# Reordering the end of the first layer norm: which plain tile comes first, which engine makes the low parts, and one square's scratch

## The chip, the cores and the metric

The kernel runs on one core of a Trainium2 chip. The metric is the device time of one execution in microseconds (us). The time before is 1299.06 us, the median of three runs.

## The reference, cut to what matters

One encoder layer over 1056 rows (1024 of a prompt, 32 of a running stream) of width 1024: a combined projection, a gated convolution beside a sparse attention, an output projection, a layer norm, an MLP with squared ReLU and a second layer norm.

```python
mix = jnp.concatenate([conv_out, attn], axis=-1) @ w_o
x = _layernorm(ALPHA * x + mix, ln1_g, ln1_b)
hid = jax.nn.relu(x @ w_ff1)
ff = (hid * hid) @ w_ff2
x = _layernorm(ALPHA * x + ff, ln2_g, ln2_b)
```

`_layernorm` subtracts the mean over the 1024 features, divides by the root of the variance plus 1e-5, and applies a gain and an offset. This case is about the first layer norm (whose result the kernel calls x1) and the start of `x @ w_ff1`.

## The kernel before

**Layout.** Features lie on partitions, rows of x on the free axis, so x is eight tiles of 128 features by 1056 columns; four buffers `z[0]` to `z[3]` hold two of them each. Columns are handled in three chunks (`CHUNKS`: 0 to 384, 384 to 768, 768 to 1056) for the output projection and the norm, and in halves of 528 and quarters of 264 for the MLP. A float32 product is made of three reduced-precision ones: every operand is split into a high part (a copy on ScalarE, `split` at L108 or its like) and a low part (raw minus high, a subtraction on VectorE or GpSimd, L111 or its like), and TensorE adds high by high, high by low and low by high (`dense` at L131 to L133, `three` at L875 to L877).

**The stretch of the change.** After the attention, the jobs in `MID` run: `w0d` the output projection of chunk 0 for the feature tile d, `lcd` the parts of the norm of chunk c, `xc` writes chunk c of x1 (`x1_out`), `tt` calls `combine_x1`, and `fce` makes the product of the plain tile e with the quarter c of x1 (`ff1`). There are four plain tiles (hidden features 14, 30, 15, 31 in groups of 128) and four quarters, so 16 products, each 24 matmuls of 264 columns over 8 feature tiles. Quarters 0 and 1 are columns 528 to 1056, quarters 2 and 3 columns 0 to 528. Quarters 2 and 3 take columns of chunk 0, which is normalised last, so ten of the products stand behind `x00` and `tt` in `MID`: four of the first two tiles (f20 f30 f21 f31), and six of the third and the fourth.

**The norm of chunk 0.** `ln_var_pe` centres each `z[i]` on VectorE (L658), squares it on ScalarE into a scratch (L660), and TensorE adds the squares over the features with a matrix of ones (`total`, L674). The scratches are named `junka`, `tie`, `rank`, `tie`, so the fourth square takes the second's place. Then come the root (L686), the reciprocal (L687), the scaling of the four buffers (L690), and `x1_out`: high parts on ScalarE (L797), gain and offset (L801), low parts on GpSimd for even tiles and VectorE for odd ones (L804), and a store of the four buffers (L806).

**The sums of x1.** The MLP's other hidden features go through a scheme of seven products instead of eight, which needs four sums of x1's blocks: t1 to t4. `combine_x1` makes them in place on VectorE (L839, L840, L841, L848; eight instructions over 128 x 1056), and `split_sum` splits each into a high part on ScalarE (L833) and a low part (L834): eight instructions of each, of which VectorE has four low parts (both of t2, the second of t3 and of t4) and GpSimd four (both of t1, the first of t3 and of t4).

**Buffers.** A product of `ff1` takes one of six PSUM buffers (`mm2`), which comes free when ScalarE has taken its ReLU (L814) and VectorE has multiplied by it (L815); the result is stored (L816). The split weights of a plain tile take two of the six places of `whl_ring`: the first tile places 0 and 1, the second 2 and 3, the third 4 and 5, and the fourth again 0 and 1, once the last product of the first tile has read them. The MLP's further steps go on round the same ring. The buffer of t4 takes the place of x1's block `12` (columns from 528, features 0 to 511), which the products of quarters 0 and 1 read.

**What sets the order.** Up to the MLP's main steps, the order of instructions on each engine is set when the program is built, by a planner that takes the instructions in the order of the program as their operands and buffers come free by its own costs. On the chip each engine then works through its list in that order and waits at the first instruction that isn't ready. In the list of TensorE, the first matmul of f22 stands right behind the first two of f03 and of f13, and takes the PSUM buffer of f20. From the MLP's main steps on (`manual_schedule`) the order of the program stands.

Of the kernel before, what the change touches and what calls it, by code (L numbers as in the profile page):

```python
# [15 lines left out]
OP = mybir.AluOpType  # L16
# [34 lines left out]
    (0, ("", "w15", "w16", "w17")),  # L51
)
MID = tuple("w00 w01 w02 x20 w03 w04 l10 l11 l12 x10 w05 w06 w07 l00 f00 f10 f01 l01 f11 f02 l02 f12 x00 tt "
            "f20 f30 f21 f31 f03 f13 f22 f32 f23 f33".split())


def native(t, g2, i0):
# [7 lines left out]
def f32(ap):  # L65
    return ap.bitcast(F32)
# [3 lines left out]
def hybrid_layer(ctx, tc, xT, win, wkw, wo, w1, w2, ckT, cv, ckiT, scT, cw, lnp, rb, cst, oh,  # L70
                 yT, kT_o, vT_o, kiT_o, pc_o, sc_o):
    nc = tc.nc
    V, S, G, PE = nc.vector, nc.scalar, nc.gpsimd, nc.tensor
# [432 lines left out]
    def st_ps():  # L506
        return psum_m.tile([128, 512], F32, name="st_b", bufs=1)
# [134 lines left out]
    def wide(name, n):  # L642
        return scr.tile([128, 768], F32, name=name).rearrange("p (a b) -> p a b", a=2)[:, :, :n]
# [8 lines left out]
            PE.matmul(mean[:, :n], ones, s1[:, a], start=(a == 0), stop=(a == 1))  # L652
        return mean

    def centred(c0, n, i, mean):

        zi = z[i][:, :, c0:c0 + n]
        V.tensor_tensor(zi, zi, mean[:, None, :n].to_broadcast([128, 2, n]), op=OP.subtract)  # L658
        sq = wide(("junka", "tie", "rank", "tie")[i], n)
        S.activation(sq, zi, AF.Square)  # L660
        return sq

    def ln_var(c0, n, add_eng, mean):
        s2 = centred(c0, n, 0, mean)
        for i in range(1, 4):
            add_eng.tensor_tensor(s2, s2, centred(c0, n, i, mean), op=OP.add)
        var = st_ps()
        for a in range(2):
            PE.matmul(var[:, :n], ones, s2[:, a], start=(a == 0), stop=(a == 1))
        return var  # L670

    def total(ps, d, a):

        PE.matmul(ps, ones, a, start=(d == 0), stop=(d == 7))  # L674

    def ln_var_pe(c0, n, mean):
        var = st_ps()
        for i in range(4):
            sq = centred(c0, n, i, mean)
            for a in range(2):  # L680
                total(var[:, :n], 2 * i + a, sq[:, a])
        return var
# [16 lines left out]
    def job(name):  # L699
        if name == "tt":  # L700
            return combine_x1()
        kind, c, d = name[0], int(name[1]), int(name[2])
        if kind == "c":
            conv_job(d)
        elif kind == "w":
            w_o_attn(d, *CHUNKS[c], w=w_first[d] if c == 0 and d < 3 else None)
            if c == 0:
                if d == 0:
                    st[0] = mm_ps()
                for e in ((d - 1, 7) if d == 7 else (d - 1,) if d else ()):  # L710
                    total(st[0][:, :CHUNKS[0][1]], e, z[e // 2][:, e % 2, :CHUNKS[0][1]])
        elif kind == "t":
            topk((d,), True)
        elif kind == "x":
            x1_out(*CHUNKS[c])
        elif kind == "f":
            if d not in first:
                first[d] = load_w(w1[CLASSIC[d]], 8, 128)
            ff1(d, first[d], QUARTERS[c])
        elif d == 0:  # L720
            if c:
                st[c] = ln_mean(*CHUNKS[c], (G if c == 2 else V))
        elif d == 1:
            st[c] = ln_var(*CHUNKS[c], (G if c == 2 else V), st[c]) if c else ln_var_pe(*CHUNKS[0], st[0])
        else:
            ln_scale(*CHUNKS[c], st[c])
# [35 lines left out]
    def part_tile(tag, dt, name):  # L762

        return (right[0] if tag == "t3" else ff).tile([128, B], dt, name=name, tag=tag)
# [11 lines left out]
    def form_part(t, o=0):  # L776
        return t[:, o:o + B].rearrange("p (a k t) -> p a k t", a=2, k=4)

    bt = {n: part_tile(n, F32R, f"b{n}") for n in ("11", "21", "22", "12")}
    xf = {n: form_part(t) for n, t in bt.items()}  # L780
# [39 lines left out]
    def combine_x1():  # L820

        early.close()
        rp = ctx.enter_context(tc.tile_pool(name="rp", side="right", reuse_waits="tile", bufs=1))
        right.append(rp)
        right.append(rp.tile([128, 4096], F32, name="at"))
        xf["t1"] = form_part(area, 0)
        xf["t2"] = form_part(area, B)
        xf["t3"] = form_part(part_tile("t3", F32R, "bt3"))
        xf["t4"] = form_part(part_tile("12", F32R, "bt4"))

        def split_sum(name, i, raw, eng):
            hi = xf[name][:, 0, 2 * i:2 * i + 2]
            S.activation(hi, raw, AF.Copy)  # L833
            eng.tensor_tensor(xf[name][:, 1, 2 * i:2 * i + 2], raw, f32(hi), op=OP.subtract)  # L834

        b11, b12 = [z[i][:, :, :H] for i in range(2)], [z[i][:, :, H:] for i in range(2)]
        b21, b22 = [z[2 + i][:, :, :H] for i in range(2)], [z[2 + i][:, :, H:] for i in range(2)]
        for i in range(2):
            V.tensor_tensor(b11[i], b12[i], b11[i], op=OP.subtract)  # L839
            V.tensor_tensor(b12[i], b22[i], b12[i], op=OP.subtract)  # L840
            V.tensor_tensor(b22[i], b22[i], b11[i], op=OP.subtract)  # L841
            split_sum("t2", i, b22[i], V)
        for i in range(2):
            split_sum("t1", i, b11[i], G)
        for i in range(2):
            split_sum("t3", i, b12[i], V if i else G)
        for i in range(2):
            V.tensor_tensor(b21[i], b21[i], b22[i], op=OP.subtract)  # L848
            split_sum("t4", i, b21[i], V if i else G)

    first = {}
    for name in MID:
# [519 lines left out]
    n = len(steps)  # L1372
# [131 lines left out]
```

## Time and profile before

| | us |
|---|---|
| median of three runs (1298.14 to 1300.75) | 1299.06 |
| the profiled execution's own time | 1297.04 |
| its span | 1295.3 |
| TensorE busy in it | 1231.1 |

The profiled execution is 2.0 us under the median of the three runs; its span is what the engines' records cover, 1.7 us less than its own time. A matmul's line in a listing carries its start, its duration, and, where the engine stood idle ahead of it, how long and which instruction let it go.

### The profile page before, as it was taken

Reading aid. Unit: us, or ns where it says so; the run is one execution under the profiler, and the core shown is the slowest. Engines: PE = TensorE matmul, PEld = TensorE weight load, DVE = VectorE, ACT = ScalarE, POOL = GpSimd, SP = SyncE. Lnnn points to the kernel's source line nnn. Section 1 sums busy time; section 2 is a strip of 40 time slices with the busy share of each in tenths; the row PEclk is TensorE's granted clock in tenths of the full one; section 3 lists DMA queues with packets and bytes.
Section 4 is the critical chain, followed back from the end, with each engine's and each line's share of the span. In section 5 each row is a group of like instructions: output and inputs, shape, how many; then the busy total and the mean of one; then the engine's idle time right before and its main releaser. Section 6 shows DMA issues by size and latency. Waiting matters only on the chain. (4 is left out here: it accounts for less than half of the span.)

```text
span 1295.3 us, 24166 instructions
## 1 busy us (share of the span) xinstructions
PE 1231.1 (95%) x8858; PEld 1193.2 (92%) x8858; DVE 943.1 (73%) x1923; ACT 693.1 (54%) x1368; POOL 620.7 (48%) x486
## 2 busy tenths in 40 slices
PE   7999999998999998899799999999999999999996
PEld 6999999998888997778799999999899999999995
DVE  5675799999568776777957676676757667767776
ACT  5666989844798888784322222222244444444344
POOL 2412355423564685563643545545444444546762
PEclk9999999999999999999899999999999999999998
DMA  6311111135631221244134443434683464464112
GB/s 210 101 67 44 34 49 43 43 114 165 178 90 19 45 71 34 74 136 145 37 114 141 142 165 126 158 130 162 249 303 101 156 211 131 134 191 131 53 55 81
DMA packets 97224, 150.01 MB, mean 116 GB/s; under 512 B 12456, under 2 KB 41808, under 8 KB 97104
## 3 DMA queue, kind: packets, MB, share of 16 engines
q1 hardware_dynamic: 81664, 139.55, 32.6%
q0 software_dynamic: 9504, 4.33, 1.9%
q10 hardware_dynamic: 5936, 4.58, 1.2%
q8 instruction: 70, 1.15, 0.4%
q14 instruction: 50, 0.41, 0.1%
HBM read 105.41 MB, written 43.00 MB: 115 GB/s over the span
## 5 line engine op out<-in xcount | busy, mean ns | idle before, releaser
L111 POOL TENSOR_TENSOR whl<-wraw,whl 128x512 fp32r<-128x512 f32 (+1 forms) x184 | 252.2, 1375 | 381.1 <-ACT whl L108 360.1
L875 PE MATMUL acc<-b,whl 128*128 128x264 f32 x1088 | 310.0, 285 | 5.4 <-DVE ring L954 2.3
L876 PE MATMUL acc<-b,whl 128*128 128x264 f32 x1088 | 310.0, 285 | 0.0
L877 PE MATMUL acc<-b,whl 128*128 128x264 f32 x1088 | 308.7, 284 | 0.0
L875 PEld LDWEIGHTS acc<-b,whl 128*128 128x128 f32 x1088 | 204.8, 188 | 6.5 <-DVE ring L954 2.5
L877 PEld LDWEIGHTS acc<-b,whl 128*128 128x128 f32 x1088 | 205.4, 189 | 0.0
L876 PEld LDWEIGHTS acc<-b,whl 128*128 128x128 f32 x1088 | 204.4, 188 | 0.0
L108 ACT ACTIVATE whl<-wraw 128x512 fp32r<-128x512 f32 (+1 forms) x184 | 113.3, 623 | 169.7 <-DVE wraw L870 141.2
L132 PE MATMUL mm<-area,whl 128*128 128x384 f32 (+4 forms) x552 | 180.9, 329 | 0.4 <-DVE area L111 0.4
L131 PE MATMUL mm<-xh,whl 128*128 128x384 f32 (+4 forms) x520 | 170.7, 330 | 9.5 <-ACT whl L108 5.3
L133 PE MATMUL mm<-xh,whl 128*128 128x384 f32 (+4 forms) x520 | 169.4, 330 | 0.0
L111 DVE TENSOR_TENSOR b<-xraw,b 128x528 fp32r<-128x528 f32 x94 | 70.5, 751 | 84.5 <-ACT b L108 84.5
L108 ACT ACTIVATE b<-xraw 128x528 fp32r<-128x528 f32 x94 | 60.6, 644 | 133.6 <-PE acc L877 74.7
L441 ACT ACTIVATE junka<-s,cand 128x1024 bf16<-128x1024 f32 (+1 forms) x93 | 96.4, 1036 | 29.7 <-DVE cand L454 23.7
L131 PEld LDWEIGHTS mm<-xh,whl 128*128 128x128 f32 (+1 forms) x520 | 97.3, 187 | 12.5 <-ACT whl L108 5.9
L132 PEld LDWEIGHTS mm<-area,whl 128*128 128x128 f32 (+1 forms) x552 | 103.5, 188 | 3.6 <-DVE area L111 0.8
L133 PEld LDWEIGHTS mm<-xh,whl 128*128 128x128 f32 (+1 forms) x520 | 97.1, 187 | 3.2 <-POOL whl L111 1.2
L111 POOL TENSOR_TENSOR whl<-at,whl 128x512 fp32r<-128x512 f32 x56 | 80.3, 1444 | 31.9 <-ACT whl L108 31.9
L443 DVE TENSOR_SCALAR_CACHE_REDUCE junk<-s,cand 128x384 bf16<-128x384 f32 (+1 forms) x124 | 80.2, 647 | 1.1
L587 POOL TENSOR_SCALAR L<-L,rs 128x1024 f32<-128x1024 f32 (+8 forms) x36 | 58.3, 1621 | 38.5 <-DVE rs L586 36.4
L875 PE MATMUL acc<-area,whl 128*128 128x264 f32 x240 | 68.6, 286 | 0.0
L877 PE MATMUL acc<-area,whl 128*128 128x264 f32 x240 | 68.2, 284 | 0.0
(327 smaller groups left out, 3344.2 us busy)
## 6 DMA issues: line engine op xcount, KB each, us to landing
hd<-ring SPq DMA_DIRECT2D x98, 264.0 KB, 2.1
xraw<-hd SPq DMA_DIRECT2D x98, 264.0 KB, 2.7
at<-in_w_dram SPq DMA_DIRECT2D x58, 256.0 KB, 3.6
wraw<-in_win_dram SPq DMA_DIRECT2D x52, 256.0 KB, 2.6
wraw<-in_wo_dram SPq DMA_DIRECT2D x40, 256.0 KB, 2.6
w_a<-in_w_dram SPq DMA_DIRECT2D x23, 256.0 KB, 3.2
w_c<-in_w_dram SPq DMA_DIRECT2D x19, 256.0 KB, 3.5
zz<-zd SPq DMA_DIRECT2D x4, 1056.0 KB, 8.5
```

The lines of the kernel that those rows point to most:

```text
L108: S.activation(hi, raw, AF.Copy)
L111: (lo_eng or G).tensor_tensor(lo, raw, f32(hi), op=OP.subtract)
L131: PE.matmul(ps, wh[k], a, start=(k == 0), stop=False)
L132: PE.matmul(ps, wh[k], b, start=False, stop=False)
L133: PE.matmul(ps, wl[k], a, start=False, stop=(k == K - 1))
L441: S.activation(junk(R, N), s, AF.Sign, bias=c, scale=-1.0, accum_out=cnt[:R, i:i + 1])
L443: V.tensor_scalar(junk(R, N), s, c, -float(k), op0=OP.is_ge, op1=OP.add, accum_out=cnt[:R, i:i + 1])
L587: G.tensor_scalar(ls[0], ls[0], rs[:R, 0:1], None, op0=OP.mult)
L875: PE.matmul(ps, wh, xhi, start=start, stop=False, skip_group_check=more)
L876: PE.matmul(ps, wh, xlo, start=False, stop=False, skip_group_check=more)
L877: PE.matmul(ps, wl, xhi, start=False, stop=stop, skip_group_check=more)
```

## The change

In `MID` the two products of the third plain tile with the quarters 2 and 3 (f22, f32) come ahead of the fourth tile's with the quarters 0 and 1 (f03, f13). In `combine_x1` all low parts of the sums are made by VectorE. In `ln_var_pe` the fourth square of chunk 0 goes to the scratch `junk`, which `ln_mean` of the chunks 1 and 2 used before, instead of `tie`; the other callers of `centred` keep their scratches.

```diff
 MID = tuple("w00 w01 w02 x20 w03 w04 l10 l11 l12 x10 w05 w06 w07 l00 f00 f10 f01 l01 f11 f02 l02 f12 x00 tt "
-            "f20 f30 f21 f31 f03 f13 f22 f32 f23 f33".split())
+            "f20 f30 f21 f31 f22 f32 f03 f13 f23 f33".split())
...
-    def centred(c0, n, i, mean):
+    def centred(c0, n, i, mean, names=("junka", "tie", "rank", "tie")):
...
-        sq = wide(("junka", "tie", "rank", "tie")[i], n)
+        sq = wide(names[i], n)
...
-            sq = centred(c0, n, i, mean)
+            sq = centred(c0, n, i, mean, ("junka", "tie", "rank", "junk"))
...
-        def split_sum(name, i, raw, eng):
+        def split_sum(name, i, raw):
             hi = xf[name][:, 0, 2 * i:2 * i + 2]
             S.activation(hi, raw, AF.Copy)
-            eng.tensor_tensor(xf[name][:, 1, 2 * i:2 * i + 2], raw, f32(hi), op=OP.subtract)
+            V.tensor_tensor(xf[name][:, 1, 2 * i:2 * i + 2], raw, f32(hi), op=OP.subtract)
...
-            split_sum("t2", i, b22[i], V)
+            split_sum("t2", i, b22[i])
         for i in range(2):
-            split_sum("t1", i, b11[i], G)
+            split_sum("t1", i, b11[i])
         for i in range(2):
-            split_sum("t3", i, b12[i], V if i else G)
+            split_sum("t3", i, b12[i])
         for i in range(2):
             V.tensor_tensor(b21[i], b21[i], b22[i], op=OP.subtract)
-            split_sum("t4", i, b21[i], V if i else G)
+            split_sum("t4", i, b21[i])
```

## Rows read from the trace of the kernel before

**Rows 1.** The page: busy time, share of the span and instructions of each engine.

```profile
PE 1231.1 (95%) x8858; PEld 1193.2 (92%) x8858; DVE 943.1 (73%) x1923; ACT 693.1 (54%) x1368; POOL 620.7 (48%) x486
```

**Rows 2.** Waits of PE from 582 us on: total, times, longest.

```profile
PE mm L131 <- DVE xraw L815: 7.7, 1, 7.7
PE acc L875 <- DVE ring L954: 2.3, 1, 2.3
PE mm L132 <- POOL b L804: 1.9, 1, 1.9
```

**Rows 3.** Stretches of the end of the norm: busy time and instructions of each engine.

```profile
core 0: us, PE busy (x) PEld busy (x) DVE busy (x) ACT busy (x) POOL busy (x), PEclk, DMA share, GB/s
...
592.40:602.40 10.00, 10.00 (x77) 9.47 (x76) 5.75 (x6) 3.37 (x7) 0.00 (x0) 1.00 0.04 14
602.40:618.90 16.50, 14.46 (x102) 13.62 (x100) 15.14 (x19) 7.05 (x11) 10.79 (x6) 0.90 0.58 192
618.90:626.60 7.70, 0.05 (x2) 0.04 (x1) 7.70 (x5) 2.74 (x6) 7.70 (x4) 0.78 0.00 0
626.60:632.90 6.30, 6.30 (x39) 6.30 (x40) 6.30 (x5) 3.53 (x6) 4.06 (x3) 0.72 0.14 46
632.90:645.30 12.40, 12.40 (x105) 12.40 (x104) 12.40 (x14) 4.28 (x9) 5.58 (x3) 1.00 0.07 25
```

**Rows 4.** Timeline of PE: start, duration, instruction, idle time before and releaser.

```profile
592.07 0.58 PE L131 MATMUL mm<-b,whl 128*128 128x264 f32 x1
...
594.55 1.45 PE L674 MATMUL st_b<-tie,cs 128*128 128x384 f32 x4
...
626.57 0.59 PE L131 MATMUL mm<-b,whl 128*128 128x264 f32 x1 [7.65 <-DVE xraw L815]
...
645.29 0.29 PE L875 MATMUL acc<-b,whl 128*128 128x264 f32 x1
```

**Rows 5.** Timeline of ACT in the same stretch.

```profile
591.33 0.84 ACT L660 ACTIVATE tie<-z 128x768 f32<-128x768 f32 x1 [2.24 <-PE st_b L674]
...
618.71 0.37 ACT L814 ACTIVATE xraw<-mm 128x264 f32<-128x264 f32 x1
...
642.59 0.39 ACT L814 ACTIVATE xraw<-mm 128x264 f32<-128x264 f32 x1 [1.98 <-PE mm L133]
645.49 0.39 ACT L814 ACTIVATE xraw<-mm 128x264 f32<-128x264 f32 x1 [2.51 <-PE mm L133]
```

**Rows 6.** Groups of DVE from 600 to 650 us: busy, mean ns of one.

```profile
L840 DVE TENSOR_TENSOR z<-z,z 128x1056 f32<-128x1056 f32 x2 | 5.8, 2924 | 0.0
...
L834 DVE TENSOR_TENSOR bt<-z,bt 128x1056 fp32r<-128x1056 f32 x2 | 4.7, 2340 | 0.0
...
L839 DVE TENSOR_TENSOR z<-z 128x1056 f32<-128x1056 f32 x2 | 2.5, 1258 | 1.4 <-POOL b L804 1.0 <-DMA zd<-z 0.3
L834 DVE TENSOR_TENSOR area<-z,area 128x1056 fp32r<-128x1056 f32 x2 | 2.4, 1247 | 0.0
```

**Rows 7.** Timeline of DVE: the first sum, two evacuations, the last low part.

```profile
610.91 1.26 DVE L839 TENSOR_TENSOR z<-z 128x1056 f32<-128x1056 f32 x1 [1.02 <-POOL b L804]
...
626.09 0.42 DVE L815 TENSOR_TENSOR xraw<-mm,xraw 128x264 f32<-128x264 f32 x1
...
639.59 0.42 DVE L815 TENSOR_TENSOR xraw<-mm,xraw 128x264 f32<-128x264 f32 x1
...
641.65 2.34 DVE L834 TENSOR_TENSOR bt<-z,bt 128x1056 fp32r<-128x1056 f32 x1
```

**Rows 8.** Groups of POOL from 600 to 650 us.

```profile
L834 POOL TENSOR_TENSOR area<-z,area 128x1056 fp32r<-128x1056 f32 x2 | 6.6, 3334 | 2.6 <-ACT area L833 2.6
```

**Rows 9.** Timeline of POOL: the fourth plain tile's second half, a weight with DVE idle.

```profile
625.01 2.29 POOL L111 TENSOR_TENSOR whl<-wraw,whl 128x512 fp32r<-128x512 f32 x1
...
649.67 1.29 POOL L111 TENSOR_TENSOR whl<-wraw,whl 128x512 fp32r<-128x512 f32 x1 [6.80 <-ACT whl L108]
```

**Rows 10.** DMA issues from 600 to 615 us: KB, median us to landing.

```profile
zd<-z SPq DMA_DIRECT2D x4, 384.0 KB, 6.3
```

## The prediction

> **What bounds the kernel now.** I read the page first: TensorE is busy for 95% of the span, so whatever is won must be idle or slow time of that engine [rows 1]. Then the waits of PE from the norm to the end: the longest single one, 7.7 us, is a matmul of L131 let go by an evacuation, L815, and 1.9 us more come from a low part of x1, L804 [rows 2]. Both lie in the stretch of the change, which I then cut into windows [rows 3].
>
> One product of `ff1` takes 2.90 us at the full clock: the ReLUs of the last two, each let go by the product's last matmul, start at 642.59 and 645.49 [rows 5]; over 24 matmuls that is 0.121 us each. The ten products behind the norm need 29.0 us. They run from 602.4 to 645.3, where the MLP's first step starts [rows 3, 4]: 42.9 us, so 13.9 us too long. The windows say where. From 602.4 to 618.9, 102 matmuls, worth 12.3 us, take 16.5: 4.2 us lost, because x1's last tiles arrive while PE already works on them. From 618.9 to 626.6 PE does almost nothing: 7.6 us lost. From 626.6 to 632.9, at a granted clock of 0.72 after that idle time, 39 matmuls worth 4.7 us take 6.3: 1.6 us lost. From 632.9 on nothing is lost; the remaining 0.5 us are the windows' edges.
>
> Before 602.4 PE is full (10.00 of 10.00 us at clock 1.00 [rows 3]), with products of quarters 0 and 1, so the ten can't begin sooner. 13.9 us is therefore all that this stretch can give back. What follows is bound by PE and moves along: the longest later wait is 2.3 us [rows 2].
>
> **The fourth square in its own scratch.** The square of `z[3]` starts at 591.33, after 2.24 us of waiting for the second square's sums [rows 5], and its four sums stand in PE's list behind some twenty matmuls of a product: 592.07 to 594.55 [rows 4]. With `junk`, whose last reader is the mean of another chunk, long done, ScalarE can square right after its two ReLUs, by about 590, and the sums can follow at 592.07. The twenty matmuls come after them instead; PE loses nothing. The whole end of the norm comes 2.5 us sooner. That is hidden up to 602.4 and then pays in the first window: at least 2.5 us of the 4.2, at most all of it, since the wait of 1.9 us [rows 2] and the reduced clock of that window (0.90 [rows 3]) shrink with it. I take 3.0, near the lower end, because later tiles still arrive one by one.
>
> **f22 and f32 ahead.** In the list, PE's wait at 626.57 [rows 4] sits on the first matmul of f22, whose PSUM buffer is f20's, and f20's evacuation runs at 626.09 [rows 7], because its ReLU waits in ScalarE's queue until 618.71 [rows 5] and VectorE is busy with sums. The fourth tile's products can't fill the time either: the low part of the second half of its weights is made by GpSimd from 625.01 for 2.29 us, behind sums' low parts [rows 9]. Moved up, f22 and f32 should get the buffers that f03 and f13 have now, free since f02 and f12, their weights have been split for long, and x1 is there. So 5.8 us of work fill the hole. The next to need f20's buffer is f03, at 602.4 + 16.5 - 3.0 + 5.8 = 621.7.
>
> **All low parts on VectorE.** GpSimd needs 3.33 us for one of its four beside a busy VectorE; VectorE needs 1.25 alone, 2.34 beside GpSimd, and its sums stretch from 1.26 to 2.92 in the same way [rows 6, 8]. The edit takes four instructions off GpSimd and adds 4 x 1.25 = 5.0 us to VectorE, whose queue also holds the evacuations. What was stretched comes back to about 1.25 each. GpSimd keeps the weights' low parts, 1.29 us each when VectorE is idle, 2.29 in the one shown beside it [rows 9]; those of the fourth tile are no longer queued behind sums and should be done before 621.7.
>
> The Trainium skill (SBUF — State Buffer, Who interferes with whom) speaks of a lock here, not of sharing: of a VectorE instruction with two inputs in SBUF and a GpSimd one that reads SBUF, the second to issue is blocked until the first ends. The stretched sums agree with that. By this rule every weight that GpSimd splits still holds VectorE up for its whole length, and an estimate with all six of them in VectorE's way would cost about 4 us more than my sum.
>
> Now VectorE's list. Its first sum starts at 610.91, set by the store of the same buffer (6.3 us to landing [rows 10]); the store moves with the norm, so 608.4. Ahead of f20's evacuation I expect eight instructions over 1056 columns (five sums; the low parts of t1 and the first of t3), 10.0 us, a low part of x1 and a weight sum, 1.2, a gap of 0.4 and the evacuation's own 0.4: 620.4 with no disturbance, 623.0 if two weights on GpSimd (1.29 each) hold it up. PE wants it at 621.7: a wait of 0 to 1.3 us, I take 1. The last of the six buffers, f31's, comes free today at 640.0 [rows 7]. Between the two evacuations stand three sums, three low parts, 7.5 us, and 1.7 of small things: 632.2, or 637.4 with four more weights in the way. f33, which needs it, is due at 621.7 + 1 + 8.7 = 631.4: 1 to 6 us; I take 2, nearer the lower end, since most of those weights can be split while PE still works on f22 and f32. Ahead of the MLP, t2 is due in its third step and t4 in its seventh, 5.8 and 17.4 us after its start, and the last low part, at 644.0 now [rows 7], should be done by 641: hidden. If it were not, each us of lateness would be one of PE. The later f13 holds block `12`, and so t4's high part on ScalarE, until about 628, which nothing on PE waits for before t4 is due.
>
> **Sum.** PE ends the ten products at 621.7 + 1 + 11.6 + 2 = 636.3 instead of 645.3: 9.0 us less, so 1288.0 for the profiled execution's 1297.04. The runs shown have a median 2.0 us higher; against it the forecast is 1290.0.
>
> **Rivals.** (a) All of it comes back: no evacuation is late, the clock stays up. 13.9 us: 1285.2. For it speaks that the undisturbed list is on time to within 1 us at both places; against it, VectorE's 5.0 us more. I count it as the forecast's lower edge. (b) The wait moves: f03 or f33 stands for 5 to 7 us in place of my 3, with another 1.6 at the lower clock, and 3 to 5 us remain: 1295. For it speaks that VectorE is full from 618.9 to 645.3 [rows 3]. (c) Nothing comes of it: the planner, whose costs I can't see, sets f20's evacuation so far back in VectorE's list that PE idles as long as now, only later: 1299. (d) The other side: with all eight low parts on VectorE, and these ahead of the products in the program, the planner puts f20's evacuation behind all of them. From 608.4: eight sums and eight low parts at 1.25 and three weight sums end at 630.7 undisturbed; at half of today's stretch on the sums, 0.8 each, at 637. Then f03, f13, f23 and f33 follow, 11.6, with 1.6 for the clock: 650, 5 us later than now: 1304. This decides from an evacuation at 632 on. Against it: today f20's evacuation stands ahead of seven of the VectorE instructions that the program names before it.
>
> **How the numbers follow.** Chances: the forecast with (a), 7 to 13.9 us won, 0.62; (b) 0.20; (c) 0.09; (d) 0.09. The range from 1285 to 1296.5 holds the first two, 0.82, with the bounds of the unknown waits. A difference under 0.2%, 2.6 us, can't be told from none here: faster 0.82, same 0.09, slower 0.09.
>
> **What would show it.** After: the fourth square's sums right behind the third's on PE, and the root 2.5 us after them no more; no wait of 7.7 us on L815; L834 on VectorE alone at about 1.25; GpSimd with weights only; the MLP's first step near 636. The prediction is wrong if f03's first matmul stands waiting for L815 past 625, if f33's stands over 6 us, or if the MLP's first steps wait for low parts of t2 or t1.

## The result, and the profile after

The changed kernel takes 1291.65 us in the median of four runs, the kernel before 1299.78 beside it; the ratio is 0.994, with a 95% interval from 0.9922 to 0.9958, so 5.5 to 10.1 us. One run of the changed kernel, 1505 us at a mean granted clock of 0.751, was disturbed and has no part in the ratio; the other three have a median of 1291.09. The profiled execution took 1292.22 us, its span is 1290.5.

The page's busy times and the waits of PE from 582 us on (total, times, longest), which answer to [rows 1, 2]:

```profile
PE 1232.6 (96%) x8858; PEld 1195.5 (93%) x8858; DVE 939.8 (73%) x1927; ACT 693.2 (54%) x1368; POOL 609.4 (47%) x482
```

```profile
PE mm L131 <- DVE xraw L815: 4.4, 1, 4.4
PE acc L875 <- DVE ring L954: 2.4, 1, 2.4
```

Four instructions went from GpSimd to VectorE, and VectorE's busy time still fell by 3.3 us. Of the two waits in the stretch of the change, that on L804 (1.9 us) is gone, and that on L815 went from 7.7 to 4.4.

The windows of the end of the norm, as in [rows 3] but cut where this kernel's waits lie:

```profile
core 0: us, PE busy (x) PEld busy (x) DVE busy (x) ACT busy (x) POOL busy (x), PEclk, DMA share, GB/s
590.40:602.90 12.50, 12.50 (x79) 10.37 (x78) 7.14 (x8) 4.16 (x10) 0.00 (x0) 1.00 0.13 43
602.90:622.05 19.15, 19.15 (x157) 18.94 (x156) 19.15 (x23) 10.52 (x18) 11.82 (x8) 1.00 0.50 166
622.05:626.45 4.40, 0.00 (x0) 0.00 (x0) 4.40 (x6) 2.07 (x4) 1.23 (x2) 0.81 0.00 0
626.45:632.40 5.95, 5.94 (x30) 5.94 (x31) 5.95 (x7) 2.09 (x4) 3.43 (x2) 0.57 0.21 70
632.40:640.50 8.10, 8.10 (x69) 8.10 (x68) 8.10 (x11) 2.97 (x4) 0.00 (x0) 1.00 0.24 84
```

The second row is to be held against the second of [rows 3]: 157 matmuls, worth 19.0 us at 0.121 each, in 19.15. Where 4.2 us were lost before, nothing is. Then PE stands for 4.4 us, and the 30 matmuls behind it, worth 3.6, take 5.95 at a granted clock of 0.57, mostly its lower level of 1.2 GHz: 2.3 us more. From 632.4 on nothing is lost. These losses make 6.8 us, where before they made 13.4 (4.2, 7.6 and 1.6). The ten products themselves take 36.2 us, from 604.31 to 640.53, instead of 42.9.

TensorE's timeline: the sums of the last two squares, f20's first matmuls, the one wait, the MLP's first step; then ScalarE's, with the fourth square, the root and f20's ReLU (compare [rows 4, 5]).

```profile
592.98 1.45 PE L674 MATMUL st_b<-rank,cs 128*128 128x384 f32 x4
594.39 1.45 PE L674 MATMUL st_b<-junk,cs 128*128 128x384 f32 x4
...
604.31 0.78 PE L131 MATMUL mm<-b,whl 128*128 128x264 f32 x5
...
626.46 0.59 PE L131 MATMUL mm<-b,whl 128*128 128x264 f32 x1 [4.41 <-DVE xraw L815]
...
640.53 0.29 PE L875 MATMUL acc<-b,whl 128*128 128x264 f32 x1
```

```profile
588.99 0.83 ACT L660 ACTIVATE rank<-z 128x768 f32<-128x768 f32 x1
589.72 0.83 ACT L660 ACTIVATE junk<-z 128x768 f32<-128x768 f32 x1
...
595.88 0.58 ACT L686 ACTIVATE rstd<-st_b,eps 128x384 f32<-128x384 f32 x1 [4.78 <-PE st_b L674]
...
615.67 0.37 ACT L814 ACTIVATE xraw<-mm 128x264 f32<-128x264 f32 x1
```

The fourth square waits for nothing, and its sums stand behind the third's, with a single matmul of a product between them. f20's ReLU is taken at 615.67. Its evacuation on VectorE comes 10.3 us later; VectorE's list shows why, and GpSimd's beside it (compare [rows 7, 9]):

```profile
610.59 1.25 DVE L839 TENSOR_TENSOR z<-z 128x1056 f32<-128x1056 f32 x1
...
614.57 1.78 DVE L870 TENSOR_TENSOR wraw<-at 128x512 f32<-128x512 f32 x1
616.27 1.25 DVE L834 TENSOR_TENSOR area<-z,area 128x1056 fp32r<-128x1056 f32 x1
617.44 2.34 DVE L840 TENSOR_TENSOR z<-z,z 128x1056 f32<-128x1056 f32 x1
619.71 2.35 DVE L834 TENSOR_TENSOR area<-z,area 128x1056 fp32r<-128x1056 f32 x1
621.98 2.31 DVE L841 TENSOR_TENSOR z<-z,z 128x1056 f32<-128x1056 f32 x1
624.21 0.68 DVE L870 TENSOR_TENSOR wraw<-wraw,at 128x512 f32<-128x512 f32 x1
624.82 1.25 DVE L834 TENSOR_TENSOR bt<-z,bt 128x1056 fp32r<-128x1056 f32 x1
625.98 1.10 DVE L815 TENSOR_TENSOR xraw<-mm,xraw 128x264 f32<-128x264 f32 x3
```

```profile
613.56 2.24 POOL L111 TENSOR_TENSOR whl<-wraw,whl 128x512 fp32r<-128x512 f32 x1 [3.31 <-PE mm L133]
616.64 2.02 POOL L111 TENSOR_TENSOR whl<-wraw,whl 128x512 fp32r<-128x512 f32 x1 [0.84 <-ACT whl L108]
618.62 2.31 POOL L111 TENSOR_TENSOR whl<-at,whl 128x512 fp32r<-128x512 f32 x1
621.50 1.68 POOL L111 TENSOR_TENSOR whl<-at,whl 128x512 fp32r<-128x512 f32 x1 [0.56 <-ACT whl L108]
```

Four weights of GpSimd fall between the first sum and the evacuation, and four of VectorE's instructions are about 1.1 us longer than their kind is alone: 2.34, 2.35 and 2.31 instead of 1.25, and 1.78 instead of 0.68.

**Which clock to read.** Executions differ in when they reach the end of the norm: the two profiles of one kernel below, that with the squaring on ScalarE, are 3.6 us apart there (585.21 and 588.79). The two profiled here differ by 1.6: the first square of chunk 0 (L660 into `junka`) starts at 585.35 before and at 586.98 after, and behind the MLP's first step both need 650.0 us. So the table below counts from that square to the first matmul of L875. It is 59.9 us before and 53.6 after: 6.4 won. (The ten products alone won 6.7; f20's first matmul stands 17.3 us behind the square, where it stood at 17.1.)

### The profile page after: what moved, and what is told of

It reads as the page before. It is cut to its first block, busy times and chain, and to the rows that moved or that the text cites. A ratio compares the mean times of both kernels' runs of the same rounds, so it can differ in the third digit from the quotient of the medians.

```text
span 1290.5 us, 24168 instructions
## 1 busy us (share of the span) xinstructions
PE 1232.6 (96%) x8858; PEld 1195.5 (93%) x8858; DVE 939.8 (73%) x1927; ACT 693.2 (54%) x1368; POOL 609.4 (47%) x482
## 5 line engine op out<-in xcount | busy, mean ns | idle before, releaser
L111 POOL TENSOR_TENSOR whl<-wraw,whl 128x512 fp32r<-128x512 f32 (+1 forms) x184 | 253.1, 1380 | 396.0 <-ACT whl L108 372.7
L875 PE MATMUL acc<-b,whl 128*128 128x264 f32 x1088 | 310.0, 285 | 5.5 <-DVE ring L954 2.4
L875 PEld LDWEIGHTS acc<-b,whl 128*128 128x128 f32 x1088 | 204.9, 188 | 6.5 <-DVE ring L954 2.6
L111 DVE TENSOR_TENSOR b<-xraw,b 128x528 fp32r<-128x528 f32 x94 | 70.6, 752 | 84.5 <-ACT b L108 84.4
L111 POOL TENSOR_TENSOR whl<-at,whl 128x512 fp32r<-128x512 f32 x56 | 81.0, 1457 | 31.3 <-ACT whl L108 31.3
L875 PE MATMUL acc<-area,whl 128*128 128x264 f32 x240 | 68.6, 286 | 0.0
```

Of the source, the lines that this page charges most:

```text
L111: (lo_eng or G).tensor_tensor(lo, raw, f32(hi), op=OP.subtract)
L875: PE.matmul(ps, wh, xhi, start=start, stop=False, skip_group_check=more)
```

## The experiments

All ratios are to the kernel before, run beside: its median was 1299.34 us beside the three single parts and the first cut of the coupling, 1298.12 beside the changed kernel's second set and the three with one part undone, 1298.31 beside the cut on the kernel before and the kernels with the squaring on ScalarE, 1300.20 beside the second set of the latter. (A ratio compares runs taken side by side and isn't quite the quotient of two medians: for the scratch alone the medians are 5.4 us apart, and the ratio says 3.6.) "To the MLP" is the time from the first square to the MLP's first matmul in the one profiled execution; the last column names PE's waits between them, over 0.4 us.

| kernel | us | ratio, interval | to the MLP | waits of PE |
|---|---|---|---|---|
| before | 1299.78 | | 59.9 | 7.65 L815; 1.9 L804 |
| changed | 1291.65 | 0.994 [0.9922, 0.9958] | 53.6 | 4.41 L815 |
| changed, again | 1291.23 | 0.9948 [0.9932, 0.9965] | 53.3 | 4.42 L815 |
| order alone | 1299.77 | 1.0008 [0.9998, 1.0018] | 59.9 | 4.45 L815; 1.86, 1.24 L804; 1.26 L111 |
| VectorE alone | 1292.16 | 0.9953 [0.9939, 0.9967] | 53.3 | 1.92, 0.43 L804; 1.61 L815; 0.51 L111 |
| scratch alone | 1293.98 | 0.9972 [0.9961, 0.9984] | 55.5 | 4.55 L815; 1.03 L111 |
| without order | 1290.65 | 0.9939 [0.9924, 0.9954] | 53.3 | 3.88 L815 |
| without VectorE | 1294.37 | 0.9969 [0.9955, 0.9983] | 55.2 | 3.84, 0.50 L815 |
| without scratch | 1291.63 | 0.9945 [0.9929, 0.996] | 52.3 | 1.24, 1.18 L804 |

**One part alone.** Each makes one of the three edits on the kernel before. The order:

```diff
-            "f20 f30 f21 f31 f03 f13 f22 f32 f23 f33".split())
+            "f20 f30 f21 f31 f22 f32 f03 f13 f23 f33".split())
```

> Of the three edits only the order of the products (f22, f32 ahead of f03, f13). Theory A (the hole in PE's work was a product standing in line for f20's PSUM buffer; two products with free buffers fill it): PE's wait on L815 falls from 7.7 us to 1 to 3 us and moves to f03, later ones of 1 to 4 us on f23 or f33 come up since VectorE's list is as long as before; 4 to 6 us less than before, about 1294.5. Theory B (the length of VectorE's and GpSimd's lists decides, whatever stands first on PE): the first MLP step starts within 1.5 us of where it did, 1298 to 1300.

No difference, to 0.2%, as theory B had it. PE no longer waits at f20's buffer, and this is what took its place (TensorE's and GpSimd's timelines of the order alone):

```profile
629.28 0.39 PE L133 MATMUL mm<-b,whl 128*128 128x264 f32 x1 [1.26 <-POOL whl L111]
...
638.11 0.59 PE L131 MATMUL mm<-b,whl 128*128 128x264 f32 x1 [4.45 <-DVE xraw L815]
```

```profile
623.49 3.49 POOL L834 TENSOR_TENSOR bt<-z,bt 128x1056 fp32r<-128x1056 f32 x1
626.94 2.28 POOL L111 TENSOR_TENSOR whl<-wraw,whl 128x512 fp32r<-128x512 f32 x1
629.19 4.57 POOL L111 TENSOR_TENSOR whl<-at,whl 128x512 fp32r<-128x512 f32 x2
```

The hole was filled, and the wait came back at a later evacuation of the same list: VectorE's sums and GpSimd's low parts were no faster, and PE meets them later, at f21's buffer. The low parts:

```diff
-            split_sum("t1", i, b11[i], G)
+            split_sum("t1", i, b11[i], V)
...
-            split_sum("t3", i, b12[i], V if i else G)
+            split_sum("t3", i, b12[i], V)
...
-            split_sum("t4", i, b21[i], V if i else G)
+            split_sum("t4", i, b21[i], V)
```

> Only the low parts of the sums on VectorE. Theory A: GpSimd is free for the low parts of the fourth tile's weights, so f03 and f13, whose buffers are free, fill the same hole with their 5.8 us; 3 to 6 us less than before, 1293.5 to 1296.5, and then the order edit adds little to it. Theory B (VectorE's and GpSimd's lists decide): the same or more, 6 to 8 us less, 1291.5 to 1293.5, and the order edit alone does nothing. Theory C (VectorE's four additional low parts stand ahead of f20's evacuation and eat the gain): 1298 to 1301.

It gives 6.1 us by itself (0.47%), most of the whole, as theory B had it. Of the wait at f20's buffer this is left:

```profile
627.60 0.39 PE L131 MATMUL mm<-b,whl 128*128 128x264 f32 x1 [1.61 <-DVE xraw L815]
```

The edit does two things at once: VectorE's sums have fewer low parts of GpSimd beside them, and GpSimd comes to the fourth tile's weights sooner. No run takes the two apart. The scratch:

```diff
...
-            sq = centred(c0, n, i, mean)
+            sq = centred(c0, n, i, mean, ("junka", "tie", "rank", "junk"))
```

> Only the fourth square's own scratch. The end of the norm comes 2.0 to 2.5 us sooner against the square sums' start. Theory A: the wait on f20's evacuation ends with VectorE's list, which starts with the norm's end, so the whole chain moves by that: 2 to 2.5 us less, about 1297.3. Rival: PE is full with products of quarters 0 and 1 up to 602.4 and the evacuation's place in VectorE's list is what counts, so nothing is won: 1299 to 1300.

It gives 3.6 us (0.28%), more than either side of the expectation had: the waits on x1's low part on GpSimd are gone, and the wait on f20's buffer, 7.65 us before, is 4.55.

**One part undone.** The changed kernel again, for a profile on the same chip, and three that each take one edit back.

> The changed kernel once more, beside the three below, so that they are compared on one chip. 7 to 9 us less than before: 1290 to 1292.

```diff
-            "f20 f30 f21 f31 f22 f32 f03 f13 f23 f33".split())
+            "f20 f30 f21 f31 f03 f13 f22 f32 f23 f33".split())
```

> The changed kernel without its first edit (f03, f13 ahead of f22, f32 again). Theory A of the first runs (the order fills the hole) would lose most of the gain, 4 to 6 us: 1295 to 1297. Theory B (the length of VectorE's and GpSimd's lists decides, and either pair of products can fill the time) loses 0 to 1.5 us: 1290.5 to 1293.

Not slower: 0.9939 beside 0.9948. The wait is there too, on the first matmul of f22 this time (timeline of TensorE):

```profile
626.49 0.59 PE L131 MATMUL mm<-b,whl 128*128 128x264 f32 x1 [3.88 <-DVE xraw L815]
```

With its low parts taken from GpSimd, the fourth tile's weights are ready early, and f03 and f13 fill the hole as well as f22 and f32 do. Without the VectorE edit (the three lines of `split_sum` back to G) and without the scratch (`tie` again):

> The changed kernel without its second edit (GpSimd makes four of the low parts again). Theory B: about what the scratch alone gave, since the order alone gave nothing: 4 to 5 us less than before, 1294 to 1296, with a wait on a late evacuation (f21's or f31's) as the order alone had it. Theory A: 7 us or more less than before, under 1292.5.

> The changed kernel without its third edit (the fourth square takes the second's place again). If the edits were independent it would give what the second alone gave, 6 us less than before, 1293; if the chain is VectorE's list from the norm's end on, the list starts 2 to 2.5 us later than in the changed kernel: 1292.5 to 1294. If the norm's end doesn't matter once the lists are short: 1290 to 1292.

Without VectorE's low parts some 3 us of the gain are lost (0.9969 beside 0.9948), and what is left equals the scratch alone (0.9972): the order adds nothing in this pair either, the third. Without the scratch the ratio is 0.9945 beside 0.9948: on top of VectorE's low parts, the scratch gives nothing that these runs can tell from zero. The same kernel beside VectorE's low parts alone (0.9953) is a fourth pair for the order, with no difference either. The interval of the first pair leaves room for 0.3 us of gain; those of the others, by an estimate from their two intervals, for 2 to 3.

**The coupling to f20's buffer cut.** The evacuation multiplies ReLU's result by the product in PSUM; taken from SBUF twice, the ReLU alone frees the buffer, and the lists of VectorE and GpSimd stay. First on the changed kernel, then on the kernel before:

```diff
-        V.tensor_tensor(r, ps[:, :n], r, op=OP.mult)
+        V.tensor_tensor(r, r, r, op=OP.mult)
```

> The changed kernel, with L815 multiplying the ReLU by itself instead of by the PSUM buffer: the same values, the same order of instructions on VectorE, but the buffer comes free with the ReLU on ScalarE (615.7 for f20) instead of with VectorE's evacuation (626.0). Theory A: the remaining wait of 4.4 us and the 2.4 us at the lower clock behind it go, the first MLP step starts 6 to 7 us sooner than in the changed kernel: 1284 to 1286. Rival: something else that depends on VectorE's list (low parts of t2, the step's weights) is late by as much, and 0 to 3 us are won: 1288 to 1291.

> The kernel before, with the factor of ReLU's square taken from SBUF instead of PSUM (r by r), so that ScalarE's ReLU alone frees a product's buffer; VectorE's and GpSimd's lists are those of before. Theory (the hole of the kernel before is the coupling of f20's buffer to VectorE's list): in before the ReLU that frees f20's buffer starts at 618.71, 7.4 us ahead of the evacuation on VectorE, so f22's matmul no longer stands for 7.65 us but for about 1 at most, and f22, f32 run on while GpSimd makes the fourth tile's weights (till 627.3); the first MLP step comes 53 to 55 us after the first square in place of 59.9, and the time is 1292 to 1295. Rival (the low parts of x1's sums and the weights on GpSimd and VectorE bind as such, not through the buffer): PE then waits for the weights or for low parts of t2 in the MLP's first steps for as long as before, and the time is 1297 to 1299.

On the changed kernel no wait is left in the ten products, and the MLP starts 46.7 us after the first square, 6.8 sooner. The time is still 1291.45 (1287.23 to 1298.30), 0.9949 [0.9927, 0.9972]: no gain that can be told. In the profiled execution 5.1 of the 6.8 us are given back behind the MLP's start. Some 3.5 of them go in its first 12 us, 64 matmuls where the changed kernel has 93, and this wait with the lower clock behind it is in that stretch (timeline and window of TensorE):

```profile
639.55 0.39 PE L875 MATMUL acc<-b,whl 128*128 128x264 f32 x1 [2.68 <-ACT ring L925]
```

```profile
636.00:645.00 9.00, 6.32 (x40) 6.11 (x39) 6.25 (x10) 3.28 (x6) 3.24 (x1) 0.81 0.27 92
```

The MLP's own evacuation on ScalarE (L925) stands behind high parts of t4, and these behind VectorE's last sums: the same list, met at another place. That is one execution of eight, whose times spread over 11 us, so what the slower ones lost isn't shown. On the kernel before, the cut gives 1295.27 us, 0.997 [0.9958, 0.9982]; the wait of 7.65 us is gone and the MLP starts at 54.0, as the coupling theory asked, with 1.39 us on a weight of GpSimd, 1.92 and 0.73 on L804 left.

**The squaring on ScalarE.** No evacuation is left in VectorE's list:

```diff
-        V.tensor_tensor(r, ps[:, :n], r, op=OP.mult)
+        S.activation(r, r, AF.Square)
```

> The changed kernel, with the squaring of ReLU's result moved from VectorE to ScalarE (Square in place of the multiplication): no evacuation stands in VectorE's list any more, which loses ten instructions of 0.35 to 0.42 us, and ScalarE's gains ten of some 0.4. Theory (PE waits in the changed kernel only since evacuations stand behind sums and low parts in VectorE's list): no wait of PE on VectorE in the ten products, the granted clock stays at 1.00 there, the first MLP step comes 46 to 48 us after the first square in place of 53.5, and the time is 1285 to 1288, unless the MLP's first steps wait for low parts, which are due then. Rival (ScalarE's list is the next to bind, as in the run where only the PSUM operand was dropped): products wait for high parts of the sums or for ReLUs, or the first MLP steps for ScalarE, and the time is 1289 to 1292, no better than the changed kernel.

The profiled execution did what the theory said: no wait in the ten products, clock 1.00, the MLP at 46.6 us, 1286.20 us. But the twelve times fell into two groups, five from 1282.01 to 1288.14 and seven from 1296.70 to 1299.98; median 1296.97, ratio 0.9961 [0.9933, 0.9989].

> The changed kernel with the squaring on ScalarE once more, since its times fell into two groups, five of 1282.0 to 1288.1 and seven of 1296.7 to 1300.0, and the profile is of the lower group. Theory (the first MLP step comes 7 us sooner in all of them, and the upper group loses it again to a lower granted clock, at a wait of TensorE that all kernels have): the times fall into two groups again, and if the profile is of the upper one, its first MLP step stands at 46 to 48 us after the first square, and some window before or behind it has a granted clock that falls where the other profile has 1.00; 10 us at half the clock are 10 to 20 us of such time. Rival (in the upper group the ten products themselves run otherwise, a wait on ScalarE that the lower group has not): the first MLP step comes 54 to 58 us after the first square, with full clock behind it.

Two groups again, seven from 1285.93 to 1289.87 and five from 1295.93 to 1300.29; median 1289.51, ratio 0.9933 [0.9911, 0.9955]. This profile is of the upper group. The rival was right in the place, since the time goes in the ten products, and wrong in the rest: the wait is on GpSimd, not on ScalarE, and the clock behind it is not full. One instruction of GpSimd, the low part of x1's last even tile, takes 1.18 us in the one profile and 10.88 in the other; each group has one profile. The lower group's GpSimd and VectorE, then the upper group's GpSimd, VectorE and TensorE (timelines):

```profile
606.94 1.18 POOL L804 TENSOR_TENSOR b<-z,b 128x384 fp32r<-128x384 f32 x1 [0.69 <-DVE z L801]
...
616.50 2.31 POOL L111 TENSOR_TENSOR whl<-at,whl 128x512 fp32r<-128x512 f32 x1
```

```profile
607.17 1.37 DVE L804 TENSOR_TENSOR b<-z,b 128x384 fp32r<-128x384 f32 x1
```

```profile
610.76 10.88 POOL L804 TENSOR_TENSOR b<-z,b 128x384 fp32r<-128x384 f32 x1 [0.69 <-DVE z L801]
```

```profile
610.99 0.55 DVE L804 TENSOR_TENSOR b<-z,b 128x384 fp32r<-128x384 f32 x1
611.46 1.25 DVE L839 TENSOR_TENSOR z<-z 128x1056 f32<-128x1056 f32 x1
...
619.54 1.25 DVE L841 TENSOR_TENSOR z<-z,z 128x1056 f32<-128x1056 f32 x1
622.91 0.69 DVE L870 TENSOR_TENSOR wraw<-wraw,at 128x512 f32<-128x512 f32 x1 [2.12 <-POOL whl L111]
```

```profile
621.69 0.59 PE L132 MATMUL mm<-b,whl 128*128 128x264 f32 x1 [8.98 <-POOL b L804]
```

VectorE goes from 610.99 to 620.79 without a pause, every instruction at its undisturbed length, and GpSimd's ends at 621.64, 0.85 us after VectorE ran out of ready work. PE waits 8.98 us and then loses 2.4 at a granted clock of 0.74 (65 matmuls worth 7.9 in 10.3 us): 11.4, where the MLP starts 11.5 later than in the lower group (58.1 to 46.6).

> The changed kernel without its new order of products (f03 and f13 ahead of f22 and f32 as before), and with the squaring moved to ScalarE as in the run beside it. If the order only says which two products stand ahead of the wait for f20's buffer, this gives the time of its neighbour within 1.5 us. If the order gives anything once the buffers are free early (f22 and f32 need no weights made in this stretch, f03 and f13 do), the neighbour is 2 us or more faster, and here PE stands for a weight of GpSimd (L111) before f03.

1295.76 us (1286.73 to 1300.75), 0.9976 [0.9956, 0.9995]. This profile shows the same on a weight:

```profile
617.38 7.35 POOL L111 TENSOR_TENSOR whl<-wraw,whl 128x512 fp32r<-128x512 f32 x1 [5.92 <-ACT whl L108]
```

```profile
624.78 0.59 PE L133 MATMUL mm<-b,whl 128*128 128x264 f32 x1 [5.32 <-POOL whl L111]
```

Here PE does wait for a weight of the fourth tile before f03, 5.32 us, as the expectation put it for the case that the order gives something; the new order has f22 and f32 in that place. Since both orders spread over more than 13 us, the medians don't decide it (of the new order's 24 times 12 are under 1290, of these 12 two), and it stays open whether the order is worth something once the buffers come free early.

## Why the prediction was right, and where it was not

The forecast was 1290.0 with a range from 1285.0 to 1296.5; the time lies inside, 1.7 us above the forecast. The mechanism holds: an evacuation that stands in VectorE's list behind sums and low parts, which GpSimd stretches. By the stretch from the first square to the MLP the sum of 9.0 us is 2.6 too high; it is made up of steps that were off in both directions, 5.7 us of loss left out at f03 and 3.2 put in elsewhere that didn't come. That the total comes this near is in part luck.

**The scratch.** Predicted: the norm's end 2.5 us sooner, worth 3.0. The root comes 8.9 us after the first square instead of 10.7, 1.8 sooner, and all 4.2 us of that window came back in the whole change. The scratch alone is worth 3.6. Right, but not a term to be added: with VectorE's low parts in place it adds nothing measurable, since PE, with its waits on L804 gone, then stands longer at f20's buffer (1.61 us with VectorE's low parts alone, 3.88 with the scratch too).

**The order: the step that failed.** "So 5.8 us of work fill the hole" credits f22 and f32 with it. In four pairs (before, scratch alone, VectorE alone, changed) the order gives nothing that the runs can tell. The sentence "The fourth tile's products can't fill the time either" was read from a trace in which GpSimd still had four low parts of sums; the second edit removes these, and the hole is filled by either pair. Without the second edit, filling it only carries the wait to 638.

**VectorE's low parts.** Predicted as a price of 1 us at f03 and 2 at f33, beside the gain that the order was credited with. They are most of the gain: 6.1 us alone. VectorE's busy time fell in spite of four more instructions, above all because the pairs L840, L841 and L848 went from 2.92, 2.73 and 2.76 us to 1.79, 2.03 and 1.24 each (groups of DVE, as in [rows 6], whose other lines are not needed here). I named this stretch and its recovery, and did not ask what it was worth without the order.

**The terms mis-sized.** f03 stood at 622.05, 35.1 us after the first square, where I had 36.4 (621.7 on the clock of before). The evacuation was to come 12.0 to 14.6 us after the first sum, the upper bound with two weights of GpSimd in the way at 1.29. It took 15.4: four weights were in the way, at 1.1 each, 4.4 us where I had at most 2.6, and the list without them is 11.0 where I had 12.0. The wait is 4.4 and not 1, with 2.3 for the clock behind it, which was not in the sum. f03's first matmul ran at 626.46, past the 625 named as a sign of being wrong; counted from the first square it is 39.5 us, and 625 was 39.7, so that sign was missed by only 0.2. On the other side f33 waits for nothing where I had 2, and the first window gave 1.2 more. The Trainium skill (SBUF — State Buffer, Who interferes with whom) would have had the weights hold VectorE up for their whole length; the rows nearly agree (2.34 beside a weight of 1.29, 1.25 alone). My estimate by it, 4 us more than the sum, had 7 us of waits at f03 and f33 together, where the sum had 3 and the trace has 4.4: nearer to the sum, since the list was shorter and f33 waited for nothing.

**The rivals.** (b), the wait that moves, is close to the trace: 4.4 us with 2.3 behind it, where (b) had 5 to 7 with 1.6. By the stretch 6.4 us are won, between the 3 to 5 of (b) and the 7 at which the forecast's share began; the interval of the ratio, 5.5 to 10.1, doesn't decide between the two. (d) needed an evacuation of f20 at 632 or later; it came at 625.98.

## What to carry to other kernels

A wait of TensorE at a PSUM buffer names the instruction that freed it, not the list that made it late: ask how long that list still is, because filling the hole with other work may only carry the wait to the list's next member, as the order alone did. When several edits meet in one list, price each with the others made, since two of them here bring the MLP's start 4.4 and 6.6 us forward alone and 6.7 together. And what a change wins in the profiled execution can be missing in others: the kernel with the lowest time, 1282 us, also had times of 1300, and only a second profile showed where.

## What the runs showed of the hardware

**A GpSimd instruction can be held off for as long as VectorE runs without a pause.** 1.18 us became 10.88, and 1.29 became 7.35, each ending about a microsecond after VectorE's run of instructions with both inputs in SBUF did. It need not be so: in the lower group VectorE's list is the same and has no pause either, yet each engine's instructions stretch by about one of the other's (GpSimd's weight 2.31 us, VectorE's L804 1.37 instead of 0.55), as they do in the kernels before and after, where GpSimd's longest L804 is 1.66 and 1.18 us. The Trainium skill (SBUF — State Buffer, Who interferes with whom) has whoever issues first keep the port for its whole instruction and the other blocked; the runs show that a blocked GpSimd need not be the next to get it. Which of the two wins isn't read from the starts: GpSimd's record starts 0.23 us ahead of VectorE's in both groups (606.94 and 607.17; 610.76 and 610.99). Nor are evacuations from PSUM in VectorE's list what lets GpSimd in, since the lower group has none there; but the times spread less with them, 1290.42 to 1294.02 for the changed kernel in its two sets of undisturbed runs, against 11 us for it with evacuations that read SBUF twice and 14 to 18 with the squaring on ScalarE. Why that is stays open.

**The granted clock after a wait.** Behind the changed kernel's 4.41 us of idle time, 30 matmuls ran at 0.57; behind 8.98 us, 65 ran at 0.74; behind 1.56 us on L925, in the lower group, none was lost (clock 1.00); behind the 1.92 us of the kernel before, the clock was 0.50 from 606.19 to 609.51. In us lost, 4.41 cost 2.3, the 7.65 of the kernel before 1.6 and 8.98 cost 2.4: a longer wait didn't always cost more.
